# A recurrent weighted average (RWKV's WKV): the order of the start-up steps and the way the twelfth tile of k is loaded

## The chip, the cores and the metric

The kernel runs on one core of a Trainium2 chip. Five engines work side by side, each in the order of its own instruction list: PE (TensorE, matrix products into PSUM), DVE (VectorE), ACT (ScalarE), POOL (GpSimd) and SP (SyncE, which only issues DMAs). They wait for each other by semaphores. An instruction that waits holds up everything behind it on its engine. The metric is the device time of one execution in microseconds (us), the median of several runs; smaller is better.

## The reference

For each of 16 sequences and 256 channels a state is carried through 2048 steps (`aa` a weighted sum of v, `bb` the sum of the weights, `pp` a running maximum that keeps the exponentials in range):

```python
for t in range(seq_len):
    ww = u + kk
    qq = np.maximum(pp, ww)
    e1 = np.exp(pp - qq)
    e2 = np.exp(ww - qq)
    output[b, t, :] = (e1 * aa + e2 * vv) / (e1 * bb + e2 + 1e-08)
    ww = pp - w + kk
    qq = np.maximum(ww, kk)
    ...
    aa = e1 * aa + e2 * vv
    bb = e1 * bb + e2
```

So the output of a step is a quotient of two weighted sums over the steps before it, plus the step's own term with the bonus u. `w`, `u` have 256 elements; `k`, `v` and the output are 16 x 2048 x 256 float32, 33.55 MB each.

## The kernel before, in words

**Tiles.** The time axis is cut into 16 groups of 128 steps (`TC`), and each group into 4 tiles of 4 sequences. Tile n (0 to 63) belongs to group c = n // 4 and holds 128 steps x 4 sequences x 256 channels, 512 KB of k and as much of v.

**Steps of a tile.** The code builds a table of named steps; the name and the tile's or the group's number are used below.

- LK n, LV n load k and v (SP for the first three tiles, POOL's queue for all others). RK n copies a k that was loaded as plain float32 (buffer `kf`) to a `kr` buffer of the type PE takes, on DVE or POOL. Tiles whose letter in `FIRST` is "C" are loaded straight into a `kr` buffer in that type (a converting load, L117) and have no RK. There are 4 `kr` buffers (`NK`) and 5 `kf` buffers (`NKP`). After `FIRST`, `PLAN` = "DDDP" says who copies: POOL for every fourth.
- For q = 0 and 1: R q n puts the rows that w and u contribute into one of two PSUM buffers X (4 products, L207); L q n adds the sums of k over time (L213); X q n takes the exponentials of it on ACT (L216) into the ring `EZR` of 11 tiles (`RING`) and so gives the X buffer back.
- CV n casts v to bf16 (L220; DVE for n < 10, POOL after that, 2 buffers), TV n multiplies the exponentials by it on DVE (L225).
- S n adds the tile's sums to the group's table TOT on PE (L252).
- DEN n and NUM n form denominator and numerator on PE (L329; DEN takes an X buffer, NUM the one buffer `num`), LN n and INV n take the reciprocal on ACT as exp(-log) (L341, L346), MUL n forms the output on DVE (L361), ST n stores it from SP.

**Steps of a group** (after its four S): CS copies the table (DVE, L258), TU turns it (PE, L265), SL takes logs (ACT, L269), FR and OF build running frames (DVE, L274 to L282), SN hands the frames on to the next group, SW takes weights (ACT, L288), CH carries the sums through (DVE, L292 and L295), KP hands them on, SS spreads the result (DVE, L302), TK turns it back (PE into TURN, L309), BK copies it to SBUF (DVE, L313). DEN and NUM of the four tiles need BK.

**Fillers.** Ahead of many PE steps `zeros` (L155) puts products of zeros into TURN. How many is written in the tables `Z0` (for tile or group 0) and `Z`, with single cases in `ZAT`. A filler may write TURN only when BK has read it.

**The order.** Each step has a place, a number in units of tiles (from the table `P`, or from `AT`, which overrides it). A planner sorts all steps by place and emits them one after the other; a step whose predecessors or buffers aren't ready is passed over and comes as soon as they are. Every engine then runs its share in exactly that order. The table `AT` is mostly about the start, where the outputs of the first tiles aren't yet due and the loads have just begun.

The order before, from S 5 on (PE and the others in one list, fillers as z): S 5, z8, TK 0, BK 0, S 6, X 1 8, TV 7, LK 12, LV 11, R 0 9, L 0 9, R 1 9, L 1 9, X 0 9, S 7, SN 0, CS 1, X 1 9, z4, TU 1, SL 1, LK 13, KP 0, CV 8, TV 8, CV 9, LV 12, FR 1, OF 1, SN 1, RK 11, RK 12, CV 10, R 0 10, L 0 10, R 1 10, L 1 10, X 0 10, X 1 10, z4, DEN 0, LN 0, INV 0, LK 14, SW 1, LV 13, z6, NUM 0, z4, R 0 11, L 0 11, R 1 11, L 1 11, X 0 11, X 1 11, LK 15, S 8, TV 9, S 9, CV 11, LV 14, DEN 1, LN 1, INV 1, MUL 0, ST 0, NUM 1, R 0 12 and so on; CH 1, KP 1 and SS 1 come after L 1 12 (each L has one filler before it, left out here).

Of the kernel before, what the change touches and what calls it, by code (L numbers as in the profile page):

```python
# [15 lines left out]
def kernel(  # L16
# [28 lines left out]
    RS = 2.0 ** -20  # L45
    CAP = 54.0
    BIG = 1e30
    FIRST = "DDDCCCCCCCC"
    VOT = 3
    XT = 8  # L50
    BYPOOL = 52
# [12 lines left out]

    AT = {"INV 55": 69.0, "SL 15": 69.1, "LN 56": 69.2, "SW 15": 75.7, "FR 15": 69.3, "TU 0": 5.01, "FR 0": 5.02,
# [4 lines left out]

    ZAT = {"DEN 0": 4, "TU 1": 4, "R 0 11": 4}

    consts = ctx.enter_context(tc.tile_pool(name="consts", bufs=1))
    kpool = ctx.enter_context(tc.tile_pool(name="kpool", bufs=NK))
# [30 lines left out]
    def how(n):  # L105
        return "D" if n < BYSP else FIRST[n] if n < len(FIRST) else PLAN[n % len(PLAN)]

# [45 lines left out]
    def zeros(m, first=False):  # L153
        for j in range(m):
            K(PE.matmul(TURN[:, 0:192], Z[:, 0:128], Z, start=first, stop=True, skip_group_check=True))  # L155
# [40 lines left out]
    X = [psx.tile([128, 2, D], F32, tag=f"X{a}", name=f"X{a}") for a in range(2)]  # L196
# [31 lines left out]
    AS, D1, L1, A0, FR, BC, A2 = range(7)  # L228
# [88 lines left out]
    RD, NUM, OT = {}, {}, {}  # L317
# [121 lines left out]
    while todo:  # L439
# [22 lines left out]
        if o["mode"] and not quiet:  # L462
            zeros(ZAT.get(" ".join(map(str, name)), P["Z0" if name[-1] < FILL else "Z"].get(name[0], 0)))
        quiet = quiet and name[0] != "BK" or name[0] == "TK"
# [32 lines left out]
```

## Time and profile before

| what | value |
|---|---|
| median of 3 runs | 288.26 us (288.19 to 288.63) |
| the profiled execution | 288.83 us, of it 287.1 us span (first to last instruction) |
| PE busy | 268.5 us (94%) |
| ACT busy | 259.0 us (90%) |
| DVE busy | 248.5 us (87%) |
| POOL busy | 175.7 us (61%) |
| DMA | 101.20 MB, mean 352 GB/s |

Busy times are those of the page's first part. The page cuts the span into 40 slices of 7.2 us: PE, ACT and DVE stand at 7 to 9 tenths from the second slice to the 36th, ACT at 6 to 8 tenths in the second to sixth. The loads run at 346 to 352 GB/s in the third to seventh slice, and loads and stores together at 353 to 394 GB/s after that. In the views below, a window's row gives its length and then, for each engine, its busy time and number of instructions; a timeline's row gives start, duration, engine, line, operation, what it writes and reads, and in brackets the engine's idle time ahead of it and what ended it.

### The profile page before, as it was taken

How to read it: one execution, taken by the hardware profiler on the slowest of the kernel's cores; microseconds unless marked ns; L12 is line 12 of the kernel's file. 1: busy time of each engine (PE TensorE's matmuls, PEld its weight loads, DVE VectorE, ACT ScalarE, POOL GpSimd, SP SyncE). 2: the span in 40 equal slices, each digit the busy share in tenths (PEclk: the TensorE clock that was granted, in tenths of full speed). 3: DMA queues.
4: the chain of work that ended last, by engine and by line, in shares of the span. 5: the costliest groups of instructions: out<-in, count | busy, mean ns of one | idle time of the engine just before them, and what ended most of it. 6: DMA issues, size and time to landing. Idle time of an engine off the chain costs nothing.

```text
span 287.1 us, 7961 instructions
## 1 busy us (share of the span) xinstructions
PE 268.5 (94%) x3215; PEld 134.8 (47%) x3215; DVE 248.5 (87%) x422; ACT 259.0 (90%) x291; POOL 175.7 (61%) x219
## 2 busy tenths in 40 slices
PE   6997999999999999999899999999999999997860
PEld 6443544454545455454445445454544454453530
DVE  5678799899898989897998989999898989889860
ACT  1786679999999999999999999999999999998990
POOL 8365476875757676874757686675766685421320
PEclk9999999999999999999999999999999999999996
DMA  6999999999999999999999999999999999955896
GB/s 220 349 351 346 349 350 352 393 382 390 381 392 389 391 392 389 389 353 388 391 393 387 381 391 388 390 376 394 383 391 369 393 391 382 369 160 142 217 275 191
DMA packets 58669, 101.20 MB, mean 352 GB/s; under 512 B 5152, under 2 KB 43688, under 8 KB 58632
## 3 DMA queue, kind: packets, MB, share of 16 engines
q0 software_dynamic: 21200, 65.42, 64.8%
q1 hardware_dynamic: 37280, 35.14, 36.5%
q8 instruction: 25, 0.41, 0.6%
q10 hardware_dynamic: 152, 0.14, 0.2%
q14 instruction: 12, 0.10, 0.1%
HBM read 67.12 MB, written 33.55 MB: 351 GB/s over the span
## 4 chain that ended last, share of the span: by engine, by line
PE 53%; DMA 23%; ACT 10%; DVE 8%; issue 3%; SPq 0%; POOL 0%; DVEq 0%; ACTq 0%; POOLq 0%
DMA out_dram<-ot 19%; PE X L213 14%; PE X L329 10%; PE num L329 8%; PE X L207 8%; PE TURN L155 7%; PE TOT L252 4%; ACT rd L341 4%; ACT EZR L216 3%; DVE ot L361 3%; DMA kr<-in_k_dram 3%; ACT rd L346 2%; DMA WUf<-in_u_dram 2%; DVE EZR L225 2%; PE TOT L265 1%
## 5 line engine op out<-in xcount | busy, mean ns | idle before, releaser
L216 ACT ACTIVATE EZR<-X 128x1024 bf16<-128x1024 f32 x128 | 126.8, 1014 | 11.5 <-PE X L213 11.5
L220 POOL CAST vb<-vr 128x1024 bf16<-128x1024 f32 x54 | 56.4, 1044 | 69.2 <-DVE EZR L225 67.8
L225 DVE TENSOR_TENSOR EZR<-EZR,vb 128x2048 bf16<-128x2048 bf16 x64 | 77.8, 1217 | 0.4
L361 DVE TENSOR_TENSOR ot<-num,rd 128x1024 f32<-128x1024 f32 x60 | 73.2, 1219 | 4.3 <-ACT rd L346 3.9
L346 ACT ACTIVATE rd<-rd 128x1024 f32<-128x1024 f32 (+1 forms) x65 | 68.0, 1046 | 2.0
L341 ACT ACTIVATE rd<-X 128x1024 f32<-128x1024 f32 (+1 forms) x65 | 65.8, 1012 | 2.9 <-PE X L329 1.1
L155 PE MATMUL TURN<-Z 128*128 128x192 bf16 x271 | 53.0, 262 | 1.5 <-DVE Z L139 1.4
L207 PE MATMUL X<-WU,CO 64*64 64x512 bf16 x512 | 51.9, 390 | 1.7 <-DVE WU L182 1.0
L121 POOL DMA_DIRECT2D vr<-in_v_dram x61 | 46.4, 761 | 7.0 <-DVE vb L220 7.0
L155 PEld LDWEIGHTS <-Z 128*128 128x128 bf16 x271 | 24.5, 101 | 50.6 <-issue 49.1
L213 PE MATMUL X<-kr,NLE 128*128 128x512 f32 x128 | 45.6, 437 | 0.7 <-DMA kr<-in_k_dram 0.7
L213 PE MATMUL X<-kr,NLZ 128*128 128x512 f32 x128 | 45.5, 436 | 0.0
L114 POOL DMA_DIRECT2D kf<-in_k_dram x53 | 40.2, 758 | 0.0
L200 DVE CAST kr<-kf 128x1024 fp32r<-128x1024 f32 x39 | 32.0, 849 | 4.2 <-DMA kf<-in_k_dram 4.0
L207 PEld LDWEIGHTS <-CO 64*64 64x64 bf16 x512 | 15.8, 104 | 32.2 <-issue 27.2
L329 PE MATMUL X<-EZR,S 64*64 64x512 bf16 x256 | 26.2, 394 | 1.7 <-ACT rd L341 1.0
L329 PE MATMUL num<-EZR,SN 64*64 64x512 bf16 x240 | 24.2, 386 | 2.2 <-DVE ot L361 2.2
L329 PE MATMUL X<-cb,Id 64*64 64x512 bf16 x256 | 25.8, 376 | 0.0
L329 PE MATMUL X<-EZR,Id 64*64 64x512 bf16 x256 | 25.8, 376 | 0.0
L252 PE MATMUL TOT<-EZR,OH 128*32 128x256 bf16 x512 | 23.7, 277 | 0.8 <-DVE EZR L225 0.5
L329 PE MATMUL num<-cb,IdN 64*64 64x512 bf16 x240 | 23.9, 376 | 0.0
L329 PE MATMUL num<-EZR,IdN 64*64 64x512 bf16 x240 | 23.9, 376 | 0.0
(69 smaller groups left out, 270.5 us busy)
## 6 DMA issues: line engine op xcount, KB each, us to landing
vr<-in_v_dram POOLq DMA_DIRECT2D x61, 512.0 KB, 7.9
kf<-in_k_dram POOLq DMA_DIRECT2D x53, 512.0 KB, 8.7
out_dram<-ot SPq DMA_DIRECT2D x64, 256.0 KB, 10.0
out_dram<-ot SPq DMA_DIRECT2D x116, 128.0 KB, 9.8
kr<-in_k_dram POOLq DMA_DIRECT2D x8, 512.0 KB, 9.5
ot<-in_k_dram SPq DMA_DIRECT2D x3, 512.0 KB, 5.2
ot<-in_v_dram SPq DMA_DIRECT2D x3, 512.0 KB, 8.4
out_dram<-ot POOLq DMA_DIRECT2D x11, 128.0 KB, 4.0
```

The source lines that it names most:

```text
L114: K((SP if n < BYSP else POOL).dma_start(out=KR[n], in_=rows_of(k, n)))
L121: K((SP if n < BYSP else POOL).dma_start(out=vr, in_=rows_of(v, n)))
L155: K(PE.matmul(TURN[:, 0:192], Z[:, 0:128], Z, start=first, stop=True, skip_group_check=True))
L207: K(PE.matmul(X[a][o:o + HS, i, :].rearrange("p (n d) -> p n d", n=2), CO[r:r + HS, q, :], WU[r:r + HS, :].unsqueeze(1).broadcast_to([HS, ...
L213: K(PE.matmul(X[a][:, i, :], (NLE, NLZ)[q], km[:, i, :], start=False, stop=True, skip_group_check=True))
L216: K(SC.activation(ez(n)[:, q, 1], X[a], ACT.Exp))
L220: K((DVE if n < EARLY else POOL).tensor_copy(vb, VR.pop(n)))
L225: K(DVE.tensor_mul(ez(n)[:, :, 0], ez(n)[:, :, 1], vb.unsqueeze(1).broadcast_to([128, 2, 2, D])))
L329: K(PE.matmul(out_tile[o:o + HS, i, :], left, right, start=s == 0, stop=s == 2, tile_position=(r, o), skip_group_check=True))
L341: K(SC.activation(RD[n][:, i], X[a][:, i], ACT.Ln, scale=RS))
L346: K(SC.activation(RD[n][:, i], RD[n][:, i], ACT.Exp, scale=-1.0))
L361: K(DVE.tensor_mul(o.rearrange("p (i n) d -> p i (n d)", i=2)[:, i], NUM[n][:, i], RD[n][:, i]))
```

## The change

The change edits three tables. `FIRST` gets a twelfth letter, so k of tile 11 comes by a converting load and RK 11 (a POOL copy) is gone. `AT` moves steps between the end of group 0's chain and the first outputs, and RK 14 and RK 16 behind it. `ZAT` puts 4 fillers ahead of TK 0 (8 before) and 2 ahead of NUM 0 (6 before).

```diff
-    FIRST = "DDDCCCCCCCC"
+    FIRST = "DDDCCCCCCCCC"
...
-          "S 6": 7.21, "S 7": 8.1, "CH 0": 6.32, "SS 0": 6.33, "BK 0": 7.21, "CV 6": 5.2, "TV 7": 7.3,
-          "KP 0": 8.6, "TV 8": 8, "R 0 6": 5.0, "R 0 8": 7.19, "R 0 9": 7.9, "CS 1": 8.2, "TU 1": 8.3,
-          "SN 0": 8.15, "FR 1": 8.95, "CV 9": 8.0, "SW 1": 9.6, "RK 11": 9.1}
-
-    ZAT = {"DEN 0": 4, "TU 1": 4, "R 0 11": 4}
+          "S 6": 7.21, "S 7": 7.215, "CH 0": 6.32, "SS 0": 6.33, "BK 0": 7.21, "CV 6": 5.2, "TV 7": 7.05,
+          "KP 0": 7.32, "TV 8": 7.8, "R 0 6": 5.0, "R 0 8": 7.19, "R 0 9": 7.2, "CS 1": 7.31, "TU 1": 7.35,
+          "SN 0": 7.3, "FR 1": 7.5, "CV 9": 8.0, "SW 1": 7.6, "RK 11": 9.1, "R 1 9": 7.22, "X 1 8": 7.1,
+          "X 1 9": 7.345, "R 0 10": 7.4, "R 1 10": 8.35, "X 1 10": 8.95, "DEN 0": 8.96, "NUM 0": 9.0,
+          "MUL 0": 9.1, "NUM 1": 10.9, "CH 1": 7.7, "S 8": 11.0, "S 9": 11.05, "CV 8": 7.33, "TK 1": 11.44,
+          "SS 1": 7.71, "X 0 10": 7.55, "RK 16": 14.3, "RK 14": 12.5}
+
+    ZAT = {"DEN 0": 4, "TU 1": 4, "R 0 11": 4, "TK 0": 4, "NUM 0": 2}
```

What the planner makes of it, from S 5 on: S 5, R 0 9, L 0 9, X 0 9, z4, TK 0, BK 0, S 6, S 7, R 1 9, L 1 9, SN 0, CS 1, KP 0, CV 8, X 1 9, z4, TU 1, SL 1, R 0 10, L 0 10, FR 1, OF 1, SN 1, X 0 10, LK 12, SW 1, CH 1, KP 1, SS 1, TV 8, LV 11, CV 9, R 1 10, L 1 10, LK 13, LV 12, X 1 10, z4, DEN 0, LN 0, INV 0, z2, NUM 0, MUL 0, ST 0, RK 12, CV 10, LK 14, LV 13, z4, R 0 11, L 0 11, R 1 11, L 1 11, X 0 11, X 1 11, LK 15, TV 9, CV 11, LV 14, DEN 1, LN 1, INV 1, NUM 1, S 8, S 9, R 0 12 and so on. TV 7 moves ahead of R 0 8, and so ahead of BK 0 on DVE. RK 14 moves from the place behind RK 13 to the place behind TV 11 and S 11, and RK 16 from ahead of DEN 4 to the place between SN 2 and TV 13. From there on the two orders are the same. PE has 8 fillers fewer, POOL one copy fewer; nothing else is added or left out.

## The prediction, made before the changed kernel ran

> **What bounds the kernel now.** I read the windows view first, over one cycle of four tiles and over the stretch in which the change acts; then the chain of waits and TensorE's timeline in that stretch, then VectorE's and GpSimd's timelines up to 60 us.
>
> ```profile
> core 0: us, PE busy (x) PEld busy (x) DVE busy (x) ACT busy (x) POOL busy (x), PEclk, DMA share, GB/s
> 30.74:45.03 14.29, 14.09 (x165) 7.32 (x168) 12.62 (x24) 10.32 (x13) 8.50 (x11) 1.00 1.12 349
> 49.46:65.64 16.18, 16.15 (x201) 7.98 (x197) 15.05 (x25) 15.94 (x19) 11.44 (x13) 1.00 1.04 388
> 65.64:81.82 16.18, 16.15 (x202) 7.98 (x197) 15.01 (x25) 15.93 (x19) 11.42 (x13) 1.00 1.05 384
> ```
>
> From 49.46 on the loop repeats every 16.18 us. PE shows work in 16.15 of it, ACT in 15.94, DVE in 15.05. So a delay of PE made before 49 us is carried to the end, and so is a gain; nothing later has room to give it back. In the stretch of the change (30.74, where S 5 begins, to 45.03, where R 0 12 begins) ACT is idle for 4 us, PE for 0.2. ACT's idle time looks like the prize, but ACT waits there for PE, which is full.
>
> ```profile
> 31.14 0.77 PE TURN L155 x8
> 31.91 0.24 PE TURN L309 x4
> 32.15 0.02 issue
> 32.17 0.70 DVE cb L313
> 32.87 0.04 issue
> 32.91 0.24 PE TURN L155
> ...
> 34.68 0.36 PE TOT L252 x8
> 35.04 0.02 issue
> 35.06 0.44 DVE ts L258
> 35.50 0.04 issue
> 35.54 0.69 PE TOT L265 x4
> ```
>
> In the chain of waits PE twice hands over to DVE and gets the work back: BK 0 copies TURN out before the next filler may write it, and TU 1 waits for CS 1. Each costs PE about 0.17 us net (R 0 9 to its filler takes 0.51 where 36.16 to 36.50 shows 0.34; the four fillers before TU 1 take 0.59 against 0.44 at 38.11). The fillers are PE time too:
>
> ```profile
> 31.07 0.83 PE L155 MATMUL TURN<-Z 128*128 128x192 bf16 x8
> 32.40 0.41 PE L207 MATMUL X<-WU,CO 64*64 64x512 bf16 x4
> 32.94 0.71 PE L213 MATMUL X<-kr,NLE 128*128 128x512 f32 x2
> 39.32 0.67 PE L155 MATMUL TURN<-Z 128*128 128x192 bf16 x6
> 45.03 0.39 PE L207 MATMUL X<-WU,CO 64*64 64x512 bf16 x4
> ```
>
> **The change on PE, up to R 0 12.** The sum is on PE's clock, from S 5 to R 0 12: 14.29 us before.
>
> Fewer fillers: TK 0 has 4 for 8, NUM 0 has 2 for 6. Eight fill 0.68 us (31.07 to 31.75), four about 0.34: twice -0.34, so -0.68. Both hand-overs above lie behind other work in the new order (S 6 and S 7 between TK 0 and the next filler; CS 1 right behind S 7, while R 1 9 and L 1 9 run): -0.35.
>
> R 0 9 now stands right behind S 5: 31.07, its filler 31.41, L 0 9 from 31.45. But L 0 9 needs the tenth k. The tile view of its load (POOL's issue at 21.77) says
>
> ```profile
> DMA to landing us min/median/max: 10.2/10.2/10.2
> ```
>
> so it lands at about 31.95. Loads land every 1.5 us there at 342 to 355 GB/s with the DMA engines full (share 1.12), and nothing ahead of this load moves, so it comes no sooner. L 0 9 starts at 32.00: +0.55.
>
> From there with the row's spacings (L to filler 0.55, four fillers 0.44, TK 0.31, S 0.33, R 0.34 and filler 0.04, L 0.64, TU 0.62): TK 0 32.99, S 6 33.30, S 7 33.64, R 1 9 33.97, L 1 9 34.35, TU 1 35.34, R 0 10 35.96, R 1 10 36.98, DEN 0 38.35, NUM 0 39.36, R 0 11 40.56, L 1 11 41.97. DEN 1 then needs X 0 11 off its buffer. X 0 11 starts at 41.69 (L 0 11 at 40.94 + 0.75) and ends at 42.71, so DEN 1 starts at 42.75 and not 42.55: +0.20. NUM 1 43.42, S 8 44.19 (from num to sums 0.77 and not 0.65: +0.1), S 9 44.52, R 0 12 44.86. Sum: -0.68 - 0.35 + 0.55 + 0.20 + 0.10 = **-0.18 us**.
>
> S 9 also waits for TV 9, which has moved behind CH 1 on DVE. SW 1 follows X 0 10 on ACT (38.02 + 0.37), CH 1 to SS 1 take 1.32 (44.07 to 45.39 before), TV 8 1.13, CV 9 0.63, MUL 0 may start when INV 0 ends (41.4) and does at 41.5, then 1.14, RK 12 0.62, TV 9 1.22: it ends at 44.48, just in time. Bounds: 0 to +0.3; I take 0. What DVE idles before FR 1 and CH 1 (1.2 and 0.4 us) was cover for TV 8 and CV 9 before.
>
> The first output: DEN 0 moves from 38.55 to 38.35, LN 0 from 39.44 to about 39.3, only MUL 0 and its store by 1.4 us. The store is off the path.
>
> **The converting load.** LK 11 goes to a kr buffer and must wait for L 1 7 (ends about 28.2) where it went out at 26.54; LV 10 behind it waits for CV 6 anyway (29.01). With 10 us of loads in flight the DMA engines don't run dry. POOL loses one cast (1.04), which nothing waited for: 0.
>
> On POOL, however, CV 10 now waits for TV 8 (40.96; 37.5 before) and CV 11 for TV 9. Behind them stand LK 14, LV 13, LK 15, LV 14, LK 16: k14 goes out at about 42.6 for 40.64, k16 at 46.6 to 47.4 for 44.81. Cover: k14 lay 7.7 us ahead of its exps, k16 9.2 (landings 47.04 and 53.66, X 0 14 at 54.73, X 0 16 at 62.81). So 0, as long as RK 16 doesn't stand where it stood.
>
> **RK 16 and RK 14.** Here is the price:
>
> ```profile
> 53.68 1.15 DVE L200 CAST kr<-kf 128x1024 fp32r<-128x1024 f32 x1 [0.17 <-DMA kf<-in_k_dram]
> 54.85 1.23 DVE L361 TENSOR_TENSOR ot<-num,rd 128x1024 f32<-128x1024 f32 x1
> 56.85 0.23 DVE L274 TENSOR_TENSOR U<-U 128x64 f32<-128x64 f32 x1 [0.77 <-ACT U L269]
> 58.12 1.22 DVE L225 TENSOR_TENSOR EZR<-EZR,vb 128x2048 bf16<-128x2048 bf16 x1
> ```
>
> Before, RK 16 sits where DVE would wait anyway (MUL 3 needs INV 3's end at 54.82; then 0.77 idle before FR 2). Moved behind SN 2 it takes 0.60 to 0.69 us straight ahead of TV 13. TV 13 ends at 59.34 and S 13 starts at 59.45, 0.07 after it may; MUL 4 behind it ends at 60.47 and NUM 5, which needs its buffer, starts at 60.52, with no slack. So PE is late by 0.60 - 0.07 = **+0.53** at S 13. ACT has 0.16 to spare at LN 5 but none at LN 6 (64.75, DEN 6 ready at 64.70), so the 0.53 stays. Bounds: 0 (covered after all) to +0.69. RK 14 moves behind TV 11, where MUL 2 waits for INV 2 (50.5): 0.
>
> **Sum:** -0.18 + 0.53 = **+0.35 us**, until the end. The profiled execution took 288.83 (span 287.1 and 1.73 around it): 289.18 by it. It lies 0.57 above the median of 288.26, so I predict 288.26 + 0.35 = **288.6**. 0.2% is 0.58 us, about what a measurement here can tell from no change.
>
> **Rivals.**
> *ACT sets the pace (faster).* Then ACT's 4 us of idle time count: INV 1 would end at 45.64 and X 0 12 start there and not at 46.63, -0.99; RK 16 costs ACT 0.53 - 0.16 = 0.37 at LN 5. Together -0.6: 287.65. For it: 15.94 of 16.18 busy. Against: L 0 12 can't start before R 0 12, whose place PE's own work sets.
>
> *DVE and POOL block each other (slower).* Place: POOL's CV 12 to RK 15 against DVE's RK 14 to FR 2. Row: the cast at 53.68 took 1.15 beside POOL's cast of 53.25, others 0.69; the scan at 38.30 took 1.11 beside POOL's cast of 38.17, others 0.36. With POOL about 2.6 us late, CV 12 falls at 49.65, ahead of RK 14 (49.93): RK 14 waits 0.76, MUL 2 0.73, and NUM 3 0.25. If v14 lands after 54.6 (estimated 53 to 54), RK 15 runs past 56.68 and FR 2 waits up to 1.04, which goes straight to TV 13. Price +0.25 to +1.04, middle 0.6: 288.26 + 0.35 + 0.6 = 289.2. Against: 0.6 to 1.5 us of room at each place by the rows.
>
> The Trainium skill, "SBUF — State Buffer", section "Who interferes with whom", says that a VectorE instruction with two SBUF inputs and a GpSimd one that reads SBUF shut each other out for a whole instruction, whoever starts first. No row here shows a TV so blocked; by the page TV 12 would stand behind CV 13 for up to 1.04 us as well, by the rows alone 0. Its time would be this rival's.
>
> *The change does less than it says* (first output hardly sooner) is part of the forecast.
>
> **Chances.** Forecast 0.45 (0.34 within 0.2%, 0.10 slower, 0.01 faster); ACT 0.22 (0.18 faster, 0.04 within); blocking 0.33 (0.28 slower, 0.05 within). So faster 0.19, same 0.43, slower 0.38. Range: from ACT's 287.65 to the blocking case's upper half, 289.4 (0.35 + 0.8): 287.6 to 289.4. The forecast's own: 288.0 (RK 16 covered) to 289.1 (TV 9 late by 0.3, RK 16 0.69).
>
> **What would show it.** L 0 9 starts at 32.0 right after a wait for the DMA; R 0 12 between 44.7 and 45.2; an idle stretch of about 0.5 on PE before S 13 near 59.5, released by TV 13; LN 6 at 65.0 to 65.3. Wrong if R 0 12 comes before 44.5 or after 45.4, if S 13 doesn't wait, or if DVE casts beside POOL's take over 1 us between 49 and 57.

## The result, and the profile after

| kernel | median | runs |
|---|---|---|
| before | 288.44 us | 6 (288.19 to 288.79) |
| changed | 289.79 us | 6 (288.87 to 289.97) |

The changed kernel takes 1.0042 times as long (95% interval 1.0026 to 1.0059): 0.0042 x 288.44 = 1.2 us slower, where 0.35 was forecast (the two medians lie 1.35 apart). Its profiled execution took 289.69 us (span 287.7).

TensorE's timeline of the changed kernel, first at the four places that the forecast named:

```profile
31.93 0.74 PE L216 MATMUL X<-kr,NLE 128*128 128x512 f32 x2 [0.36 <-DMA kr<-in_k_dram]
...
44.38 0.41 PE L210 MATMUL X<-WU,CO 64*64 64x512 bf16 x4
...
53.49 0.41 PE L332 MATMUL num<-EZR,SN 64*64 64x512 bf16 x4 [1.52 <-DVE ot L364]
...
60.05 1.00 PE L255 MATMUL TOT<-EZR,OH 128*32 128x256 bf16 x16
```

In the kernel before, the last two of these are

```profile
52.48 0.39 PE L329 MATMUL num<-EZR,SN 64*64 64x512 bf16 x4
...
59.12 0.67 PE L252 MATMUL TOT<-EZR,OH 128*32 128x256 bf16 x16
```

L 0 9 starts at 31.93 after a wait for its k, as forecast. R 0 12 starts at 44.38, 0.65 sooner than before and 0.48 sooner than the 44.86 of the forecast: the early part gains more than I had worked out. Then NUM 3 waits 1.52 us for MUL 2. Before, NUM 3 doesn't wait, and no NUM of that trace waits longer than 0.76. The last row holds S 12 and S 13: together 1.00 and not the 0.67 of before (RK 16's delay).

The windows view of the changed kernel (length; busy time and instructions of each engine; clock; DMA share; GB/s) over the cycle in which that happens, the cycle after it, and one earlier stretch:

```profile
core 0: us, PE busy (x) PEld busy (x) DVE busy (x) ACT busy (x) POOL busy (x), PEclk, DMA share, GB/s
49.46:65.64 16.18, 14.56 (x172) 6.81 (x170) 14.53 (x23) 14.65 (x17) 12.35 (x14) 1.00 1.04 384
65.64:81.82 16.18, 16.16 (x205) 7.97 (x197) 14.87 (x25) 15.83 (x19) 11.47 (x14) 1.00 1.05 383
...
44.00:46.00 2.00, 2.00 (x29) 0.94 (x22) 1.72 (x3) 1.84 (x3) 2.00 (x3) 1.00 0.74 187
```

In one cycle PE works 14.56 of 16.18 us, where it worked 16.15 before; one cycle later it is full again. So 1.6 us go between 49 and 66 and never come back. The loss is not spread over the loop. The chain of waits of the changed kernel (start, duration, what) says what is in it:

```profile
49.02 0.78 issue
49.80 2.51 DVE kr L203
52.30 1.14 DVE ot L364
53.44 0.04 issue
53.49 0.84 PE num L332 x12
```

One cast of VectorE, RK 14, takes 2.51 us. In the kernel before, 26 of the 39 casts of its kind take about 0.69, and none more than 1.40. VectorE's timeline of the changed kernel shows it with its neighbours TV 11 and MUL 2:

```profile
48.67 1.21 DVE L228 TENSOR_TENSOR EZR<-EZR,vb 128x2048 bf16<-128x2048 bf16 x1
49.80 2.51 DVE L203 CAST kr<-kf 128x1024 fp32r<-128x1024 f32 x1
52.22 1.21 DVE L364 TENSOR_TENSOR ot<-num,rd 128x1024 f32<-128x1024 f32 x1
```

Before, the first of these rows is RK 13 and RK 14 together, the second MUL 2:

```profile
48.49 1.28 DVE L200 CAST kr<-kf 128x1024 fp32r<-128x1024 f32 x2
...
50.83 1.22 DVE L361 TENSOR_TENSOR ot<-num,rd 128x1024 f32<-128x1024 f32 x1
```

GpSimd's timeline of the changed kernel, with CV 10, LK 14, CV 11, LK 16, and CV 12 and CV 13 in one row:

```profile
40.60 1.43 POOL L223 CAST vb<-vr 128x1024 bf16<-128x1024 f32 x1 [4.43 <-DVE EZR L228]
41.98 1.20 POOL L117 DMA_DIRECT2D kf<-in_k_dram  x1
...
44.66 1.38 POOL L223 CAST vb<-vr 128x1024 bf16<-128x1024 f32 x1
...
46.73 0.75 POOL L117 DMA_DIRECT2D kf<-in_k_dram  x1
...
49.04 2.71 POOL L223 CAST vb<-vr 128x1024 bf16<-128x1024 f32 x2
```

And GpSimd's timeline of the kernel before, with the same casts CV 10 to CV 13, and then CV 14 and RK 15:

```profile
39.65 1.04 POOL L220 CAST vb<-vr 128x1024 bf16<-128x1024 f32 x1 [0.45 <-DMA vr<-in_v_dram]
40.64 0.75 POOL L114 DMA_DIRECT2D kf<-in_k_dram  x1
...
43.08 1.04 POOL L220 CAST vb<-vr 128x1024 bf16<-128x1024 f32 x1 [0.15 <-DVE EZR L225]
...
47.03 1.05 POOL L220 CAST vb<-vr 128x1024 bf16<-128x1024 f32 x1
50.98 1.04 POOL L220 CAST vb<-vr 128x1024 bf16<-128x1024 f32 x1 [2.89 <-DVE EZR L225]
...
53.25 1.04 POOL L220 CAST vb<-vr 128x1024 bf16<-128x1024 f32 x1 [0.53 <-DVE EZR L225]
54.23 1.50 POOL L200 CAST kr<-kf 128x1024 fp32r<-128x1024 f32 x1
```

CV 10 waits for TV 8 now (idle 4.43, ended by line 228), and everything on GpSimd behind it is 1 to 2 us late: k14 goes out at 41.98 (40.64 before), k16 at 46.73 (44.81). CV 12 and CV 13, 4 us apart before, run as one block from 49.04 to 51.75. RK 14 "starts" at 49.80, while CV 12 runs, and ends at 52.30, 0.55 after the block. That fits a cast that does its work when both are through: in every run a VectorE cast that starts beside an earlier GpSimd cast ends 0.54 to 0.62 behind a GpSimd cast. Note where such a wait is booked: inside the duration of the instruction. No idle time is shown ahead of RK 14.

What is unusual is that RK 14 waited for both casts. Ten times in the trace before and ten times in that of the changed kernel a VectorE cast is served between two GpSimd casts that follow each other without a gap. The last two rows above are such a pair: RK 16 (53.68, 1.15 long) ends at 54.83, 0.54 behind the first, and it is the second that waits and takes 1.50. Among the VectorE casts of all runs that began while the first of such a pair had more than 0.1 to go, only RK 14 of the changed kernel and of e6 (run 7 below) was passed over. Both times CV 12 had itself waited for TV 11 (it takes 1.72 for 1.04; in the changed kernel TV 11 ends at 49.87), and the second cast was a CV, where in all the other pairs it is an RK. Which of the two is the reason, or whether it is another, isn't shown.

To compare executions I use one measure throughout: the start of the exp X 0 n minus that of X 0 8, less the same figure of the kernel before, both of the profiled execution. It leaves out that X 0 8 itself lies up to 1.4 us apart in them. Positive is later than before:

| us against before | X 0 13 | X 0 14 | X 0 16 | X 0 18 | X 0 24 |
|---|---|---|---|---|---|
| changed kernel | -0.57 | +0.64 | +1.20 | +1.30 | +1.29 |
| RK 14 back (e1) | -0.60 | +0.44 | +0.86 | +0.95 | +0.95 |
| before + RK 14 moved (e4) | +0.19 | +0.18 | +0.18 | +0.18 | +0.16 |
| short casts (e7) | -0.62 | -0.62 | +0.54 | +0.64 | +0.98 |
| RK 14 behind MUL 2 (e8) | -0.56 | -0.57 | -0.14 | -0.05 | +0.78 |
| e8, loads ahead (e12) | -0.28 | -0.28 | +0.50 | +0.59 | +0.58 |
| TV 8 sooner (e6) | -0.52 | +0.64 | +1.19 | +1.28 | +1.27 |
| e12, RK 16 ahead (e11) | -0.22 | -0.22 | +0.39 | +0.48 | +0.47 |
| CV 12 ahead (e13) | -0.16 | -0.15 | +1.30 | +1.42 | +1.42 |
| e13, RK 16 ahead (e15) | -0.42 | -0.06 | +1.40 | +1.50 | +1.50 |
| e15, loads ahead (e14) | -0.54 | -0.55 | -0.54 | -0.55 | -0.20 |
| before + RK 16 moved (e5) | +0.02 | +0.01 | +0.44 | +0.53 | +0.54 |
| before + extra store (e9) | +0.30 | +0.29 | +0.29 | +0.29 | +0.69 |

The early gain is -0.57; at X 0 15 the changed kernel is +1.03 late, so 1.60 is lost around RK 14; from there to X 0 18 another 0.27. I use positions up to X 0 24 for mechanisms and medians for the time, since single executions of one kernel end up to 2.4 us apart (before: 287.5 to 289.9 in 35 runs), and a profiled one can lie 1.6 from its kernel's median (e13: 290.99 for 289.4). Before's own profiled execution, for one, loses some 0.7 near X 0 36 to a late k (RK 36 waits 1.70), which the changed kernel's doesn't, so that only +0.54 of the +1.30 is left at the end of these two.

The levels in the table scatter too. Up to X 0 13 the kernels e4, e5 and e9 have the order of before, and yet read +0.19, +0.02 and +0.30. The ten kernels with the changed start read -0.16 to -0.62 there; in all but e6 the spread is there at X 0 9 already, which waits for a k whose landing doesn't move with X 0 8. So changes along a row tell more than its level; two levels that differ by 0.3 or 0.4 can be scatter.

### The profile page after: what moved, and what is told of

Same layout as the page of the kernel before. It is cut to its first block, busy times and chain, and to the rows that moved or that the text cites. A ratio compares the mean times of both kernels' runs of the same rounds, so it can differ in the third digit from the quotient of the medians.

```text
span 287.7 us, 7944 instructions
## 1 busy us (share of the span) xinstructions
PE 268.7 (93%) x3207; PEld 134.6 (47%) x3207; DVE 248.1 (86%) x422; ACT 259.2 (90%) x291; POOL 176.7 (61%) x218
## 4 chain that ended last, share of the span: by engine, by line
PE 70%; DVE 8%; ACT 8%; DMA 7%; issue 4%; POOL 2%; DVEq 0%; POOLq 0%; ACTq 0%
PE X L216 17%; PE X L332 14%; PE num L332 12%; PE X L210 9%; PE TURN L158 9%; PE TOT L255 6%; DMA vr<-in_v_dram 4%; DMA kr<-in_k_dram 4%; ACT rd L344 3%; DVE ot L364 3%; ACT EZR L219 2%; ACT rd L349 2%; DVE EZR L228 2%; PE TOT L268 2%; DVE kr L203 1%
## 5 line engine op out<-in xcount | busy, mean ns | idle before, releaser
L223 POOL CAST vb<-vr 128x1024 bf16<-128x1024 f32 x54 | 57.8, 1070 | 70.6 <-DVE EZR L228 70.6
L124 POOL DMA_DIRECT2D vr<-in_v_dram x61 | 46.6, 764 | 4.0 <-DVE vb L223 4.0
L203 DVE CAST kr<-kf 128x1024 fp32r<-128x1024 f32 x39 | 32.8, 867 | 3.2 <-DMA kf<-in_k_dram 3.2
```

The source lines that it names most:

```text
L124: K((SP if n < BYSP else POOL).dma_start(out=vr, in_=rows_of(v, n)))
L223: K((DVE if n < EARLY else POOL).tensor_copy(vb, VR.pop(n)))
```

## The experiments

The theory: RK 14 is shut out by two late casts of GpSimd. Its rivals: RK 14's new place alone costs the time; the late loads do; RK 16 does. Edits are of `AT` in the changed kernel unless "before" is said; of a long line some edits show only the part that changes.

**1. RK 14 back behind RK 13 (e1).**

```diff
-          "SS 1": 7.71, "X 0 10": 7.55, "RK 16": 14.3, "RK 14": 12.5}
+          "SS 1": 7.71, "X 0 10": 7.55, "RK 16": 14.3}
```

> The changed kernel with RK 14 back right behind RK 13 (RK 16 stays behind SN 2). Blocking theory (POOL's two casts CV 12 and CV 13, late by 2 us, run beside RK 14 and stretch it from 0.69 to 2.51 us; MUL 2 and then NUM 3 wait 1.5): RK 14 now runs at about 48.5, ahead of TV 11, it takes 0.7 to 1.2, NUM 3 waits under 0.3 on MUL 2, X 0 14 starts at 54.0 to 54.3 (55.26 in the changed kernel, 54.73 before), and the median falls by about 1.1 us against the changed kernel, to 288.3 to 288.8. Rival (RK 16's place is the loss): X 0 14 comes no earlier than 55.0, the median stays at 289.5 or more. Rival (late loads are the loss): RK 14 now waits for the fifteenth k, which landed at 48.38, and TV 11 behind it, so NUM 3 waits as long.

289.83 us, 1.0048 of before (1.0025 to 1.0071): no recovery. VectorE's timeline of this kernel:

```profile
49.09 1.58 DVE L203 CAST kr<-kf 128x1024 fp32r<-128x1024 f32 x1 [0.32 <-DMA kf<-in_k_dram]
50.59 1.21 DVE L228 TENSOR_TENSOR EZR<-EZR,vb 128x2048 bf16<-128x2048 bf16 x1
```

Here RK 14 waits for its k, which went out late (42.01) and landed at 49.06, and then for CV 12 (it ends 0.56 behind it); now it holds up TV 11 (50.59, in the changed kernel 48.67), and S 11 waits 0.76 for that. In the old place the same lateness of GpSimd is paid in another coin. While GpSimd is late, RK 14 escapes it in neither of these two places. The forecast of the blocking theory missed: NUM 3 doesn't wait, but RK 14 takes 1.58, X 0 14 starts at 55.10 and the time stays. By its end this run can't tell the theory from the rivals; the next three do.

**2. Before, with RK 14 moved alone (e4).**

```diff
-          "SN 0": 8.15, "FR 1": 8.95, "CV 9": 8.0, "SW 1": 9.6, "RK 11": 9.1}
+          "SN 0": 8.15, "FR 1": 8.95, "CV 9": 8.0, "SW 1": 9.6, "RK 11": 9.1, "RK 14": 12.5}
```

> The kernel before with RK 14 alone moved behind TV 11. Blocking theory: POOL's casts are not late here (CV 12 at 47.0, CV 13 at 51.0), so RK 14 at about 50.2 stands alone, takes 0.7, MUL 2 starts by 51.0, NUM 3 waits 0.3 at most, and the time is the one before, 288.3 to 288.8. Rival (RK 14's place itself is wrong, whatever POOL does): RK 14 takes over 1.5 or NUM 3 waits over 1 us, and the time rises by 1 us or more.

288.32 us against 288.32 (1.000, 0.9983 to 1.0018). VectorE's timeline of this kernel:

```profile
50.13 0.69 DVE L200 CAST kr<-kf 128x1024 fp32r<-128x1024 f32 x1
50.73 1.22 DVE L361 TENSOR_TENSOR ot<-num,rd 128x1024 f32<-128x1024 f32 x1
```

With GpSimd on time the move costs nothing, as forecast: 0.69, and MUL 2 isn't late. (The steady +0.18 in the table is there before RK 14.) It stood alone by little: CV 13 came at 50.28, 0.15 behind RK 14, and was the one that waited (1.44).

**3. The casts CV 12 and CV 13 made short (e7).** The computation is changed: only the first of four sequences of v is cast in these two tiles, and TV 12 and TV 13 multiply all four by it.

```diff
-        K((DVE if n < EARLY else POOL).tensor_copy(vb, VR.pop(n)))
+        m = slice(0, 1) if n in (12, 13) else slice(0, 4)
+        K((DVE if n < EARLY else POOL).tensor_copy(vb[:, m], VR.pop(n)[:, m]))
...
+        if n in (12, 13):
+            one = VB.pop(n)[:, 0:1, :].unsqueeze(1).broadcast_to([128, 2, 4, Dm])
...
```

> The changed kernel, in which CV 12 and CV 13 cast only the first of the tile's four sequences (a quarter of the columns) and TV 12 and TV 13 multiply by that one for all four; the outputs of those tiles and of what follows them are not the reference's. Blocking theory: POOL's two casts shrink from 2.7 to about 0.7 us together, RK 14 from 2.51 to 0.7 to 1.0, NUM 3 waits under 0.3 us, X 0 14 starts at 54.0 to 54.3. Rival (RK 14 is slow for another reason, its place, its data or its buffer): RK 14 still takes over 2 us and NUM 3 waits over 1 us.

VectorE's timeline of this kernel:

```profile
50.19 0.69 DVE L203 CAST kr<-kf 128x1024 fp32r<-128x1024 f32 x1 [0.75 <-DMA kf<-in_k_dram]
50.80 1.22 DVE L370 TENSOR_TENSOR ot<-num,rd 128x1024 f32<-128x1024 f32 x1
```

Casts of 0.4 us: RK 14 is back at 0.69, and X 0 14 comes 1.26 sooner than in the changed kernel (-0.62 for +0.64). That shows the block as the cause of the first and largest loss. The one time taken, 289.94, shows no gain at the end. X 0 16 is at +0.54 again: RK 16 stands in its late place here too, and data come late (CV 14 waits 2.15 for its v); how the loss divides between them isn't shown.

**4. RK 14 behind MUL 2 (e8).**

```diff
-"RK 14": 12.5}
+"RK 14": 12.9}
```

> The changed kernel with RK 14 behind MUL 2 instead of ahead of it. Blocking theory: MUL 2, which reads one operand from PSUM, starts at about 49.9 to 50.2 beside POOL's casts and is not stretched; RK 14 behind it starts at about 51.1 when the casts are nearly done and takes 0.7 to 1.2; NUM 3 doesn't wait; X 0 14 at 54.0 to 54.4, median 288.3 to 288.9. If MUL 2 is stretched too, the casts block whatever DVE runs, and X 0 14 stays at 55 or later.

289.18 us, 1.0023 (1.0004 to 1.0041). VectorE's timeline of this kernel:

```profile
49.87 1.23 DVE L364 TENSOR_TENSOR ot<-num,rd 128x1024 f32<-128x1024 f32 x1 [0.16 <-ACT rd L349]
51.01 1.13 DVE L203 CAST kr<-kf 128x1024 fp32r<-128x1024 f32 x1
...
71.14 1.00 DVE L203 CAST kr<-kf 128x1024 fp32r<-128x1024 f32 x1 [1.79 <-DMA kf<-in_k_dram]
```

GpSimd runs the same block (48.88, 2.71 us for both), but MUL 2, whose num comes out of PSUM, isn't held up by it, and RK 14 takes the rest of the block behind it. The gain survives to X 0 14 and X 0 15 (-0.57 both); RK 16's place takes 0.43 up to X 0 16. Then something new: RK 20 waits 1.79 for k20, and X 0 24 is at +0.78. So late loads are a third part of this kernel's loss, and its median misses the forecast of 288.3 to 288.9. In the changed kernel k20 lands at the same time (71.17, here 71.11) but RK 20 waits only 0.33, because the work is late itself: these costs don't add, the later of work and data decides.

**5. Before, with an extra store of 512 KB behind ST 0 (e9),** to see what room the loop has for DMA time: tile 0's output goes also to tile 60's place, which is overwritten later.

```diff
+        if n == 0:
+            c, p = divmod(60, 4)
+            for h in (0, 2):
+                K(SP.dma_start(out=out[4 * p + h:4 * p + h + 2, c * TC:(c + 1) * TC, :].rearrange("n t d -> t n d"), in_=OT[n][:, h:h + 2, :]))
```

> The kernel before with one more 512 KB store behind ST 0 (tile 0's output goes to tile 60's place too, where the right one overwrites it later). Theory L (the loads set the pace of the loop, the DMA engines being full from 4 us on): the 512 KB take 1.3 to 1.5 us of the DMA engines' time, k16 and k20 land that much later (53.66 and 69.87 before), RK 16 or RK 20 on DVE waits for them over 1 us, X 0 24 starts 0.5 to 1.4 us later, and the median rises by 0.5 to 1.4 us. Theory C (PE and ACT set it and 9 us lie between a k's landing and its exponentials): X 0 24 moves by under 0.25, the median by under 0.3.

288.5 us, 1.0014 (0.9996 to 1.0032): the interval holds 1. k20 landed at 71.03 (69.87 before) and RK 20 waited 1.31; X 0 24 is 0.40 later than X 0 18 would have it. An extra 512 KB (1.3 us at 390 GB/s) is felt, but only in part: the 0.40 lies between the two theories' forecasts.

**6. The loads ahead of the late cast (e12).** e8 with k14, k15 and k16 issued ahead of CV 10.

```diff
-"RK 14": 12.5}
+"RK 14": 12.9, "LK 14": 9.17, "LK 15": 9.18, "LK 16": 9.19}
```

> The changed kernel with RK 14 behind MUL 2 (as in the run before) and LK 14, LK 15, LK 16 ahead of CV 10 on POOL, so that they don't wait for TV 8. Theory L: the DMA engines stay full between 42 and 46 us (over 330 GB/s, 187 to 215 before), k14 lands by 47.2 and k20 by 70.2, RK 20 waits under 0.6 us, so the lead of 0.9 us at X 0 14 loses only RK 16's 0.4 and stays at 0.2 to 0.5 us at X 0 24; median 0.6 to 1.2 us under the run with RK 14 behind MUL 2 alone. Theory C: the order of the loads is of no account, X 0 24 is as in that run (+0.5), the median within 0.3 of it.

288.89 us, 1.0021 (1.0002 to 1.004). The DMA stretch from 44 to 46 us is full again (340 GB/s for 187 in the changed kernel), RK 20 waits 0.20, and nothing is lost between X 0 18 and X 0 24: the late loads are shown as the cause of that part. The median isn't the forecast 0.6 to 1.2 under e8's (1.0021 for 1.0023). For here TV 11 runs into CV 12. VectorE's timeline of this kernel:

```profile
48.68 2.05 DVE L228 TENSOR_TENSOR EZR<-EZR,vb 128x2048 bf16<-128x2048 bf16 x1
```

A TV takes 2.05 where all 64 of before take 1.21 to 1.23. TV 12 does the same beside CV 13, and X 0 16 is at +0.50. The 0.3 by which X 0 13 lies behind the changed kernel's is there at X 0 9 already, and so is scatter and not this edit's.

**7. TV 8 sooner (e6),** to have GpSimd on time.

```diff
-"TV 8": 7.8, "R 0 6": 5.0,
+"TV 8": 7.335, "R 0 6": 5.0,
...
-"CV 9": 8.0, "SW 1": 7.6,
+"CV 9": 7.65, "SW 1": 7.6,
```

> The changed kernel with TV 8 back ahead of FR 1, and CV 9 between SW 1 and CH 1, so that POOL can start CV 10 when v10 lands (39.4) and not at TV 8's end (40.6); RK 14 and RK 16 stay as changed. If POOL's lateness is the root of both losses: LK 14 goes out at 40.5, CV 12 ends ahead of RK 14, which takes under 1.2 us (2.51), NUM 3 waits under 0.4, DMA moves over 300 GB/s at 44 to 46 us, X 0 14 starts at 54.0 to 54.4 and X 0 24 by 0.5 us or more earlier than in the changed kernel; median 288.5 to 289.2. If it is not, RK 14 still takes over 2 us.

289.75 us, 1.0051 (1.0033 to 1.007). GpSimd's timeline of this kernel:

```profile
40.05 1.04 POOL L223 CAST vb<-vr 128x1024 bf16<-128x1024 f32 x1 [3.54 <-DVE CB L305]
```

It doesn't come on time: CV 10 starts right behind SS 1 (39.99), 0.5 after its v has landed, and only 0.55 sooner than in the changed kernel; why it waits for that isn't shown. CV 11 then takes 1.97 beside TV 10. CV 12 and CV 13 still run as one block and RK 14 takes 2.50. One thing this does tell: the loads from 44 to 46 us ran at 358 GB/s, and the lag is that of the changed kernel (+1.27 at X 0 24). So in the changed kernel itself the thin stretch of loads costs nothing on top of the block. As a test of GpSimd's lateness the run failed, since it left GpSimd late (CV 12 at 49.33).

**8. e12 with RK 16 between MUL 3 and FR 2 (e11).**

```diff
-"RK 16": 14.3, "RK 14": 12.9, "LK 14": 9.17
+"RK 16": 14.04, "RK 14": 12.9, "LK 14": 9.17
```

> The changed kernel with the loads ahead of CV 10, RK 14 behind MUL 2, and RK 16 between MUL 3 and FR 2, where DVE waits for SL 2. If RK 16's place costs what its length says, the 0.4 us at X 0 16 are saved as well: X 0 16 starts at 61.8 to 62.2, X 0 24 at 94.3 to 94.9 (95.17 before), median 287.5 to 288.1, faster than before by 0.2 to 0.8 us. If theory L holds and the loads can't follow, the lead at X 0 16 is lost by X 0 24 through RK 20's wait, and the median is the one before.

288.04 us against 288.15, 1.0002 (0.9986 to 1.0017): the time before. TV 11 and TV 12 still take 2.05 each, X 0 16 comes at 63.34 where 61.8 to 62.2 was forecast, and the gain of 0.57 isn't seen.

**9 to 11. CV 12 taken out of the block (e13, e15, e14).** In the changed kernel CV 12 goes ahead of LK 16, LV 15 and LK 17 on GpSimd, and CV 13 behind TV 12 as before; then RK 16 as in e11; then k14 and k15 ahead of CV 10.

```diff
-"RK 16": 14.3, "RK 14": 12.5}
+"RK 16": 14.3, "RK 14": 12.5, "CV 12": 11.3, "TV 12": 12.92, "CV 13": 12.93}
```

The last line in e15, and in e14:

```diff
+"RK 16": 14.04, "RK 14": 12.5, "CV 12": 11.3, "TV 12": 12.92, "CV 13": 12.93}
```

```diff
+"RK 16": 14.04, "RK 14": 12.5, "CV 12": 11.3, "TV 12": 12.92, "CV 13": 12.93, "LK 14": 9.17, "LK 15": 9.18}
```

> The changed kernel with one thing mended: CV 12 stands right behind LV 14 on POOL, ahead of LK 16, LV 15 and LK 17 (TV 12 and CV 13 keep their places on DVE and POOL). From X 0 8 on, X 0 14 takes 24.90 us in the kernel before and 25.55 in the changed one, X 0 24 takes 65.34 and 66.63. Blocking theory: CV 12 runs by 46.7 to 47.8 beside MUL 1 and BK 1, CV 13 comes behind TV 11's end, RK 14 takes under 1.2 us (2.51), NUM 3 waits under 0.3 and X 0 14 falls at 24.2 to 24.5 after X 0 8; RK 16 then costs 0.4 to 0.6, and what the loads cost shows at RK 20 (0.3 to 0.8 if the thin stretch at 44 to 46 us is felt there): X 0 24 at 65.2 to 65.9. If RK 14 is as slow as before, POOL's casts are not its cause.

> The run with CV 12 early, and RK 16 between MUL 3 and FR 2 in place of behind SN 2. If RK 16's place costs 0.4 to 0.6 as its length says, X 0 16 falls at 32.2 to 32.6 after X 0 8 (32.98 before, 34.18 in the changed kernel). With the loads as they are (thin at 44 to 46 us) RK 20 waits over 1 us and X 0 24 gives back 0.3 to 1.0: 65.0 to 65.6. If it gives back nothing, the loads are not a cause.

> As the run before it, and LK 14 and LK 15 ahead of CV 10. If three causes (casts beside RK 14, RK 16's place, thin loads) are all, the early gain is kept: X 0 16 at 32.2 to 32.6 and X 0 24 at 64.6 to 65.0 after X 0 8, the median 0.3 to 0.8 us under the kernel before, 287.4 to 287.9. If the loop has no room for a lead at all, X 0 24 comes back to 65.3 and the median is that of before.

e13: 289.4 us, 1.0021 (0.9998 to 1.0044). e15: 289.43, 1.0027 (1.0009 to 1.0045). With CV 12 out of the way RK 14 takes 0.70 and 0.90, as forecast, but it waits 0.81 and 1.02 us for k14, and in e15 RK 16 waits 1.41 for k16 too; X 0 24 misses both forecasts (+1.42 and +1.50). With the block gone, late loads take its place at once. k14 goes out only 0.3 to 0.4 later than in the changed kernel but lands 2.4 later (50.77 and 50.78 for 48.38); why its way takes so long isn't shown. e14, with the loads out in time: 288.13 against 288.41, 0.9987 (0.9968 to 1.0006). VectorE's timeline of e14:

```profile
50.09 0.69 DVE L203 CAST kr<-kf 128x1024 fp32r<-128x1024 f32 x1
50.69 1.22 DVE L364 TENSOR_TENSOR ot<-num,rd 128x1024 f32<-128x1024 f32 x1
...
55.95 0.68 DVE L203 CAST kr<-kf 128x1024 fp32r<-128x1024 f32 x1
...
86.68 1.45 DVE L203 CAST kr<-kf 128x1024 fp32r<-128x1024 f32 x1 [0.86 <-DMA kf<-in_k_dram]
```

RK 14, MUL 2 and RK 16 take their usual time (TV 12 takes 2.13 beside CV 13, which no later exp shows), and the early gain reaches X 0 18 whole (-0.55 for -0.57 of the changed kernel at X 0 13). With all three causes taken out the changed kernel's loss is gone (its interval, 1.0026 to 1.0059, lies wholly above this one). But RK 24 then waits 0.86 for its k, and -0.55 shrinks to -0.20: here the loads can't follow work that is ahead. That this version beats the kernel before isn't shown (the interval holds 1).

**12. Before, with RK 16 moved alone (e5).**

```diff
-          "SN 0": 8.15, "FR 1": 8.95, "CV 9": 8.0, "SW 1": 9.6, "RK 11": 9.1}
+          "SN 0": 8.15, "FR 1": 8.95, "CV 9": 8.0, "SW 1": 9.6, "RK 11": 9.1, "RK 16": 14.3}
```

> The kernel before with RK 16 alone moved behind SN 2. The prediction's sum for this step: S 13 waits for TV 13 about 0.53 us, X 0 16 falls at 33.3 to 33.6 after X 0 8 (32.98 before), X 0 24 at 65.7 to 65.95 (65.34), median +0.35 to +0.7. Rival (the slot ahead of MUL 3 wasn't free, and MUL 3 gains what TV 13 loses): X 0 24 within 0.15 of before.

288.89 us against 288.41, 1.0015 (0.9999 to 1.0032). TensorE's timeline of this kernel:

```profile
61.04 0.40 PE L252 MATMUL TOT<-EZR,OH 128*32 128x256 bf16 x6 [0.37 <-DVE EZR L225]
```

S 13 waits 0.37 for TV 13, X 0 16 is at +0.44, X 0 18 at +0.53, X 0 24 at +0.54: RK 16's place costs in the profile what was worked out for it. The interval of the time just holds 1.

## Why the prediction was wrong

It failed at one step: "RK 14 moves behind TV 11, where MUL 2 waits for INV 2 (50.5): 0". The step holds for a GpSimd that is on time (e4: nothing lost). The forecast itself had CV 10 and CV 11 late, and yet the step's 0 was worked out on VectorE's side alone; that CV 12 would then lie on RK 14 was seen, but only priced as a rival. In the changed kernel RK 14 lay against both, took 2.51 us, and the work lost 1.60 up to X 0 15; with the casts made short 1.26 of it was back at X 0 14 (e7).

The others in order:

- *The early part, -0.18:* -0.57 to X 0 13 (-0.65 for R 0 12). It fell outside its bounds of 44.7 to 45.2, and under the 44.5 that was named as a sign of being wrong. The signs of the terms were right. The tenth k did hold up L 0 9 (0.36 booked, at 31.93 for 32.00). What was off were spacings taken from rows with other neighbours: four fillers take 0.34 ahead of TK 0 and TU 1 and not the 0.44 that they take ahead of DEN 0 (which they still do), S 6 with S 7 0.55 and not 0.67, TU 1 0.54 and not 0.62, S 8 with S 9 0.58 and not 0.67. That is 0.10 + 0.10 + 0.12 + 0.08 + 0.09 = 0.49; L 0 9 came 0.07 sooner, and the other spacings give 0.08 back, which makes the 0.48. Two of these were on hand in the kernel before: S 8 and S 9, behind each other, took 0.55 there, and four fillers ahead of TK 1 took 0.34.
- *S 9 behind TV 9, 0:* right; S 9 has no wait.
- *The converting load, 0:* right for the load itself (k11 landed at 37.86, 38.04 before). What was put behind it, the loads that GpSimd issues late, is half wrong. The issues came about as forecast (k14 at 41.98 for "about 42.6", k16 at 46.73 for "46.6 to 47.4"), but the DMA engines did run dry: 187 GB/s from 44 to 46 us. In the changed kernel that is hidden behind RK 14's delay (e6). Where the delay is gone it costs 0.83 at RK 20 (X 0 24 against X 0 18 in e8), and nearly nothing with the loads ahead of CV 10 (e12).
- *RK 16, +0.53:* right when alone (e5: +0.44 at X 0 16, +0.53 at X 0 18). In the changed kernel 0.27 is seen between X 0 15 and X 0 18, behind work that is already late. LN 6 came at 65.94 where 65.0 to 65.3 was named.
- *"So is a gain":* the loop was said to carry a gain to the end as it carries a delay. The loads don't let it: in e8 and in e14 work that is ahead waits for its k (1.79 and 0.86).
- *The first output:* MUL 0 at 41.06 for 42.94 before, 1.9 sooner where 1.4 was forecast; off the path, as said.

With the sizes measured the sum is -0.57 + 1.60 + 0.27 = +1.30, which is X 0 18's place in the table, and the ratio of the times gives 1.2.

The rival that came true is "DVE and POOL block each other": its mechanism and its place (CV 12 against RK 14) are the ones found, and its test (casts over 1 us between 49 and 57) spoke. Its price was mis-sized. It had RK 14 wait 0.76 and NUM 3 0.25, for one cast; the runs show 1.8 (2.51 - 0.69) and 1.52, because CV 13 follows CV 12 without a gap and RK 14 doesn't get in between. That price was fair by the rows of before, where a VectorE cast is served after one cast. But the rival's row "others 0.69" was read too kindly: nine of the 39 casts of before took 1.12 to 1.40, RK 16 among them, so that the test had been met before the change, too. It also had RK 15 and FR 2 as the dearer half, which cost nothing here. The Trainium skill, "SBUF — State Buffer", section "Who interferes with whom", says that whoever comes first holds the shared ports for its whole instruction. CV 12 (1.72 us, while TV 11 ran until 49.87) and RK 14 agree with it; that the one who has waited is passed over a second time is seen at RK 14 alone.

"ACT sets the pace" would have X 0 12 0.99 sooner, and it came 1.12 sooner (45.51 for 46.63). But that lead isn't kept: LN 2 then waits 0.33 for TensorE, and X 0 13 comes 0.69 sooner, just as TensorE's own R 0 13 does (48.77 for 49.46). So TensorE set the pace.

What stays open: whether the loop can hold any lead at all, since its loads already wait; how much of the changed kernel's 1.2 us would come back by each cause alone, as one covers the other (e1, e6, e13 and e15 take out one or two and get nothing that can be told from the changed kernel's time); why RK 14 was passed over between CV 12 and CV 13; and whether e14 beats the kernel before.

## What to carry to other kernels

When an edit makes one engine later, cost every move on the other engine against the *new* times of the first, row by row, and look for instructions that come to lie against each other without a gap. Look for such waits in durations that are a multiple of their kind's usual one, since the idle times don't show them. Where, as here, the DMA engines are full nearly throughout, a delay of work and a delay of loads can cover each other, so take all suspected causes out together once before judging any of them by the end time.

## What the hardware showed that I had not expected

- A VectorE cast beside an earlier GpSimd cast ended 0.54 to 0.62 behind it. As a rule of these traces it was served before the next GpSimd cast, which then took 1.50 for 1.04 (ten times before). RK 14 was not: 2.51 us for 0.69, beside a block of 2.71.
- A bf16 multiplication of VectorE with both inputs in SBUF took 1.95 to 2.13 us for 1.21 beside a GpSimd cast that had started first (e11, e12, e14, e15); the multiplication with one input in PSUM took its usual 1.23 beside the same casts (e8). Where VectorE's instruction had started first, GpSimd's casts stretched, from 1.04 to 1.4, 1.72 and 1.97, and ended 0.9 behind it.
- A stretch of 2 us in which the loads ran at 215 GB/s (e8; 344 before) showed 25 us later, as a wait of 1.79 us for one k; with the loads of that stretch at 340 (e12) the wait was 0.20.
